# Attention value products as direct fp32 matmuls of 64 columns, low parts moved by DMA

## The chip, the cores and the metric

The kernel runs on one core of a Trainium2 chip. The metric is the time of the program on the device in microseconds (us). The core has a matrix engine (TensorE, PE in the rows; PEld is its weight loads), a vector engine (VectorE, DVE), a scalar engine (ScalarE, ACT), GpSimd (POOL), and SyncE (SP), which here only issues DMAs. Each engine executes its own list of instructions in order and waits on semaphores for the others.

## The reference

Two layers over 256 tokens of width 1024. Layer 0 is a gated linear recurrence, layer 1 attention; each is followed by a squared-ReLU MLP of width 4096. All is fp32. The change lies in layer 1:

```
proj  = h @ w_in                  # q (16 heads of 64), 6 k/v sets (4 groups of 64), 48 gates
k_c   = gelu(flat(k blocks) @ w1_k) @ w2_k          # "compressed" keys, 15 blocks of 32 tokens
v_c   = gelu(flat(v blocks) @ w1_v) @ w2_v
for each head h of group g (4 heads a group):
    p_c = softmax(q k_c^T - slope * distance)       # 15 columns
    p_s = softmax(q k_s^T - slope * distance)       # causal; all 4 blocks are selected
    p_w = softmax(q k_w^T - slope * distance)       # causal; the window covers all 256 tokens
    o_h = gate0 * p_c v_c + gate1 * p_s v_s + gate2 * p_w v_w
x = x + concat(o) @ w_out
```

## The kernel before

Everything is stored transposed: `xt` holds the residual as 8 chunks of 128 features by 256 tokens. An fp32 product is made of three fp32r products. An operand is split into a high part (a copy rounded to fp32r, `hi`) and a low part (the difference, `lo`), and `mm3` (L307) issues hi·hi, hi·lo and lo·hi into the same accumulator. The weights stream from HBM in 512 KB pieces into 5 raw buffers, are split by ScalarE (`whi`) and VectorE (`wlo`, L313), and are used once.

The attention layer is one `Section`: its parts call `add` with an engine, a planned duration, what they read and what they write, and a wished time `t`; `Plan.emit` (L202) orders them on every engine by list scheduling with those planned durations. So the order of the instructions is fixed when the kernel is built. `TSTAGE` and `FPS` set the wished times: one head every `TSTAGE` us, with `FPS` quarter-projections of "filler" work for TensorE between.

The section first makes the projections of the compressed branch (`cproj`), its hidden layer (`hidden`, L884: 96 matmuls with 64 weight columns and 62 streamed columns), the first keys (`kchunk`), the values of the two other branches (`values`) and the first queries (`qchunk`). Then 16 heads go through it:

- `scores` (L1050): products of queries and keys for the two query halves and both branches (128x256 and 128x512). VectorE adds the ALiBi matrix and takes the maximum (L1075); ScalarE takes the exponential with its row sum (L1078). The query tiles `sa` and `sb` hold the high part of one head in one half of the partitions and its low part in the other half, so one matmul over 128 partitions does both parts.
- `rescale` (L1082): VectorE turns the sum into gate/sum (L1087, L1088, L1090) and multiplies `pt` by it as a broadcast tensor (L1096).
- `transposes` (L1100): TensorE transposes the probabilities; ScalarE makes `pth` (L1111), VectorE the low part `ptl` (L1112).
- `pv` (L1116), once for two heads: the weight tile `vhl` holds the high and the low part of the values side by side (64 + 64 columns), and `pth` and `ptl` are streamed through it (L1138, L1140), beside the compressed branch (L1127). The two halves of the 128 output rows are added by a ScalarE copy and a VectorE add (L1144, L1147), and the sum is split into `oh` and `ol` for the output projection.

The query and key projections of the later heads and the first half of the output projection (`out_t`) are the fillers. The second half of the output projection and the first three pieces of the second MLP end the section.

Of the kernel before, what the change touches and what calls it, by code (L numbers as in the profile page):

```python
# [19 lines left out]
P = 128  # L20
# [11 lines left out]
NPT, NTH = 3, 4  # L32
TSTAGE, FPS = 4.4, 3.0
# [18 lines left out]
def weight_pieces():  # L52

    order = []
    order += [{"c": ("in", 8 + i), "y": ("in", i)}[k] for k, i in RG_ORDER if k != "g"]
    order += [("out", m) for m in range(8)]
    order += mlp_pieces(0)
    order += [("ck", 0), ("ck", 1), ("cv", 0), ("cv", 1), ("ks", 0), ("kw", 0), ("w1k", 0), ("w1v", 0)]
# [10 lines left out]
GATES = [("gate", i) for i in range(4)]  # L69
# [150 lines left out]
def trunk_kernel(ctx: ExitStack, tc: tile.TileContext, x_in, vec_in, const_in, w2_in, wts, out):  # L220
# [556 lines left out]
    with ExitStack() as ph:  # L777
# [18 lines left out]
        osumt = at.tile([P, 2, S], F32, name="osum")  # L796
        osum = [osumt[:, i] for i in range(2)]
# [3 lines left out]
        ptht, ptlt = (at.tile([P, NTH * 3 * P], F32R, name=n) for n in ("pth", "ptl"))  # L801
        pth, ptl = ([x[:, i * 3 * P:(i + 1) * 3 * P] for i in range(NTH)] for x in (ptht, ptlt))
        add("pool", 1.74, lambda e: e.memset(kl.bitcast(F32), 0.0), w=["kl"], t=-9)
        add("pool", 0.15, lambda e: e.memset(kc.bitcast(F32), 0.0), w=["kc0"], t=-9)

        ti = {"n": 0}

        def qchunk(c, b, t, step):
            z, zk = proj_t("q", c, b, t, step)
            t += 4 * step  # L810
            n = ti["n"] = ti["n"] + 1
            x, xk = tt[n % 3], ("tt", n % 3)
# [4 lines left out]
            add(HI, copy(a[:64], x[:64]), r=[xk], w=[ak], t=t + 0.5)  # L817
            add(HI, copy(b_[64:], x[64:]), r=[xk], w=[bk], t=t + 0.5)
            add("dve", 0.34, diff(a[64:], x[:64], a[:64]), r=[xk], w=[ak], t=t + 1)
            add("dve", 0.34, diff(b_[:64], x[64:], b_[64:]), r=[xk], w=[bk], t=t + 1)  # L820

        def kchunk(gp, br, b, t, step):
            z, zk = proj_t(("ks", "kw")[br], gp, b, t, step)
            t += 4 * step
            n = ti["n"] = ti["n"] + 1
            x, xk = tt[n % 3], ("tt", n % 3)
            add("dve", 0.34, lambda e: e.tensor_tensor(x, z(), rs, op=OP.mult), r=[zk, "rs"], w=[xk], t=t)
            cs = slice(br * S, (br + 1) * S)
            for hf in range(2):
                own, oth, g = own_(hf), own_(1 - hf), gp * 2 + hf  # L830
                gk = ("k", g, br)
                add(HI, copy(kh[own, g, cs], x[own]), r=[xk], w=[gk], t=t + 0.5)
                add(HI, copy(kh[oth, g, cs], x[own]), r=[xk], w=[gk + (1,)], t=t + 0.5)
                add("dve", 0.34, diff(kl[own, g, cs], x[own], kh[own, g, cs]), r=[xk, gk, "kl"], w=[gk + (2,)],
                    t=t + 1)
# [9 lines left out]
        zhs = [zv(oht, i * 4 * S) for i in range(2)]  # L845
        zls = [zv(olt, i * 4 * S) for i in range(2)]
        zpt = [[("pt", i, qc, b) for i in range(NPT) for qc in range(2) for b in range(2)]] * 2
        zok = [[(n, 4 * i + j) for n in ("oh", "ol") for j in range(4)] for i in range(2)]
        hvk = [(n, i) for n in ("pth", "ptl") for i in range(NTH)]
        w2h = pre.tile([64, 192], F32R, name="w2h")  # L850
        w2l = pre.tile([64, 192], F32R, name="w2l")
        cb = [pre.tile([64, 2], F32, name="cb%d" % i) for i in range(2)]
        hid = [pre.tile([64, 4, NCP], F32, name="hid%d" % i) for i in range(2)]
        hkh = pre.tile([64, 4 * NCP], F32R, name="hkh")
        hkl = pre.tile([64, 4 * NCP], F32R, name="hkl")
        hvh, hvl = (x[:64, :512].rearrange("p (a b f n) -> p a b f n", a=4, b=4, f=2) for x in (ptht, ptlt))
        bd = osumt.rearrange("p a (j e) -> p a j e", j=4)
        add("act", 0.25, copy(w2h, w2raw), w=["w2h"], t=2)
        add("dve", 0.3, diff(w2l, w2raw, w2h), r=["w2h"], w=["w2l"], t=2)
# [7 lines left out]
        def cproj(i, gp, b, t, step):  # L867
            z, zk = proj_t(("ck", "cv")[i], gp, b, t, step)
            t += 4 * step
            for hf in range(2):  # L870
                g = gp * 2 + hf
                own = own_(hf)
                dst = zfs[i][:, g * NB:(g + 1) * NB].rearrange("p n l -> p (n l)")
                for j in range(2):
                    add("dve", 0.34, lambda e, dst=dst, own=own, j=j: e.tensor_tensor(
                        dst[own_(j)], z()[own, j * 16:j * 16 + 240], rs[own, j * 16:j * 16 + 240], op=OP.mult),
                        r=[zk, "rs"], w=[("zf", i, g, j)], t=t + 0.1 * j)

        def csplit(i, t):
            keys = [("zf", i, g, j) for g in range(4) for j in range(2)] + [("zf", i, "p"), ("zf", i, "z")]  # L880
            add([("act", 0.95, 0.0), ("dve", 0.6, 0.5)], copy(zhs[i], zfs[i]), r=keys + zpt[i], w=[("zh", i)] + zok[i], t=t)
            add("dve", 1.1, diff(zls[i], zfs[i], zhs[i]), r=keys + zpt[i] + [("zh", i)], w=[("zl", i)] + zok[i], t=t)

        def hidden(i, b, t):  # L884
            wh, wl, wk = weight("w1k" if i == 0 else "w1v", 0, t)
            hp = zview(("hp", i), b, lambda x: x[:64])
            for q_ in range(4):
                def run(e, q_=q_):
                    for l in range(4 * q_, 4 * q_ + 4):
                        w = slice(l * 64, (l + 1) * 64)  # L890
                        mm3(hp()[:, :ZW], wh[:, w], wl[:, w], zhs[i][:, :, l], zls[i][:, :, l], l == 0, l == 15)
                add("pe", 0.61, run, r=wk + zok[i] + [("zh", i), ("zl", i)], w=[("ps", b)], t=t + 0.7 * q_)
            t += 3
# [5 lines left out]
        def kc_out(t):  # L899
            hf_ = hid[0].rearrange("p g n -> p (g n)")  # L900
            add("act", 0.2, copy(hkh, hf_), r=[("hid", 0)], w=["hkh"], t=t)
            add("dve", 0.15, diff(hkl, hf_, hkh), r=[("hid", 0), "hkh"], w=["hkl"], t=t)
            o = zview("kco", 6, lambda x: x[:, :4 * NCP])
            add("pe", 0.33, lambda e: mm3(o(), w2h[:, :P], w2l[:, :P], hkh, hkl, True, True),
                r=["w2h", "w2l", "hkh", "hkl"], w=[("ps", 6)], t=t)
            o4 = lambda: o().rearrange("p (g n) -> p g n", g=4)
            add("act", 0.1, lambda e: e.copy(kc[:, :, 0], o4()), r=[("ps", 6), "kc0"], w=["kch"], t=t)
            for hf in range(2):
                own = own_(hf)
                add("dve", 0.1, lambda e, own=own, hf=hf: e.tensor_tensor(  # L910
# [3 lines left out]
        def vc_out(t):  # L914
            bc = lambda g: hid[1][:, g, None, :].to_broadcast([64, 8, NCP])
            part = lambda x, g: x[:, g // 2 * 2:g // 2 * 2 + 2, :, g % 2].rearrange("p a b n -> p (a b) n")
            for g in range(4):
                add("act", 0.2, copy(part(hvh, g), bc(g)), r=[("hid", 1)] + hvk, w=[("hvh", g)], t=t)
                add("dve", 0.2, diff(part(hvl, g), bc(g), part(hvh, g)), r=[("hid", 1), ("hvh", g)] + hvk, w=[("hvl", g)],
                    t=t)  # L920
            o = zview("vco", 7, lambda x: x[:, :4 * 64].rearrange("p (a e) -> p a e", a=4))

            def run(e):
                for a in range(4):
                    lh, ll = (x[:, a].rearrange("p b f n -> p (b f n)") for x in (hvh, hvl))
                    mm3(o()[:, a], lh, ll, w2h[:, P:], w2l[:, P:], True, True)
# [423 lines left out]
```

## Time and profile before

| | |
|---|---|
| median of three timed runs | 605.43 us (605.3 to 605.85) |
| span of the profiled execution, first to last instruction | 602.2 us |
| what lies around the span (median less span) | 3.2 us |
| TensorE, VectorE, ScalarE busy | 96%, 75%, 59% of the span |
| weights read from HBM | 99.2 MB, mean 166 GB/s |
| attention section on TensorE | about 263 to 417 us, then the second MLP |

Busy times are sums over instructions. TensorE overlaps its matmuls, so the length of one (about 280 ns for 256 columns) is longer than the time to the start of the next (about 115 ns), and a wait that is shorter than the difference does not show as idle. The profiled execution's own total is not listed apart from its span; the 3.2 us around it are taken as fixed.

### The profile page before, as it was taken

The page shows a single profiled execution, that of the slowest core. Times are in us where ns is not written, and L with a number is a line of the kernel's source. Part 1 is how long each engine was busy: PE and PEld are TensorE (multiplying, and loading weights), DVE is VectorE, ACT ScalarE, POOL GpSimd, SP SyncE. Part 2 cuts the span into 40 slices and gives each one's busy share as a digit, 9 for nine tenths or more (in the row PEclk, how much of TensorE's full clock was granted, in tenths as well). Part 3 has the DMA queues.
Part 4 walks back from the last instruction along what each step waited for, and adds up shares of the span by engine and source line. Part 5 has one row for each costly group of instructions (what it writes and reads, how often), then busy time and mean ns, then how long its engine had stood idle before and what let it go on. Part 6 is the DMA issues. An engine that isn't in the chain of part 4 may idle for free.

```text
span 602.2 us, 12254 instructions
## 1 busy us (share of the span) xinstructions
PE 578.5 (96%) x4835; PEld 563.7 (94%) x4835; DVE 448.7 (75%) x921; ACT 355.0 (59%) x684; POOL 46.7 (8%) x57
## 2 busy tenths in 40 slices
PE   8999999999999999999999877899999999999994
PEld 7999999999999999999998765789999999999994
DVE  6999997767674564669999998999876667364432
ACT  7799586666563343446778766686666565253310
POOL 2110000000001221310010000000000000142220
PEclk9999999999999999999999988899999999999997
DMA  8933676555556556453730021116676667656402
GB/s 296 372 132 106 210 245 211 198 187 203 185 208 210 177 194 221 167 190 124 275 106 2 0 82 60 53 57 205 215 215 199 189 198 215 208 170 208 149 1 71
DMA packets 29178, 101.07 MB, mean 168 GB/s; under 512 B 3376, under 2 KB 4016, under 8 KB 29120
## 3 DMA queue, kind: packets, MB, share of 16 engines
q1 hardware_dynamic: 28512, 99.70, 50.0%
q8 instruction: 38, 0.62, 0.4%
q10 hardware_dynamic: 576, 0.53, 0.3%
q14 instruction: 20, 0.16, 0.1%
q0 software_dynamic: 32, 0.05, 0.0%
HBM read 99.22 MB, written 1.05 MB: 166 GB/s over the span
## 4 chain that ended last, share of the span: by engine, by line
PE 76%; DVE 19%; ACT 2%; issue 1%; DMA 1%; SPq 0%; DVEq 0%
PE bank L309 24%; PE bank L308 24%; PE bank L310 24%; DVE wlo L313 3%; DVE ptl L1112 2%; DVE pt L1096 2%; DVE pt L1075 2%; DVE xb L627 2%; DVE osum L1147 1%; DMA xt<-in_dram 1%; PE bank L950 1%; PE bank L951 1%; PE bank L952 1%; DVE t L679 1%; PE bank L1140 1%
## 5 line engine op out<-in xcount | busy, mean ns | idle before, releaser
L308 PE MATMUL bank<-hhl,whi 128*128 128x256 f32 x768 | 215.1, 280 | 1.9 <-DVE tt L815 1.0
L310 PE MATMUL bank<-hhl,wlo 128*128 128x256 f32 x768 | 213.0, 277 | 0.4 <-DVE wlo L313 0.4
L309 PE MATMUL bank<-hhl,whi 128*128 128x256 f32 x768 | 213.1, 277 | 0.1
L308 PEld LDWEIGHTS bank<-hhl,whi 128*128 128x128 f32 x768 | 144.6, 188 | 3.0 <-DVE tt L815 1.4
L277 DVE TENSOR_TENSOR wlo<-raw,whi 128x1024 fp32r<-128x1024 f32 x115 | 143.9, 1272 | 2.2 <-ACT whi L268 2.2
L310 PEld LDWEIGHTS bank<-hhl,wlo 128*128 128x128 f32 x768 | 144.4, 188 | 0.8 <-DVE wlo L313 0.8
L309 PEld LDWEIGHTS bank<-hhl,whi 128*128 128x128 f32 x768 | 144.5, 188 | 0.6 <-DVE hhl L540 0.3
L308 PE MATMUL bank<-uhl,whi 128*128 128x256 f32 x512 | 141.7, 277 | 0.0
L309 PE MATMUL bank<-uhl,whi 128*128 128x256 f32 x512 | 141.7, 277 | 0.0
L310 PE MATMUL bank<-uhl,wlo 128*128 128x256 f32 x512 | 141.6, 277 | 0.0
L268 ACT CAST whi<-raw 128x1024 fp32r<-128x1024 f32 x116 | 118.0, 1039 | 23.1 <-issue 18.8
L308 PEld LDWEIGHTS bank<-uhl,whi 128*128 128x128 f32 x512 | 96.2, 188 | 0.0
L310 PEld LDWEIGHTS bank<-uhl,wlo 128*128 128x128 f32 x512 | 96.1, 188 | 0.0
L309 PEld LDWEIGHTS bank<-uhl,whi 128*128 128x128 f32 x512 | 96.1, 188 | 0.0
L313 DVE TENSOR_TENSOR wlo<-raw,whi 128x1024 fp32r<-128x1024 f32 (+2 forms) x76 | 81.3, 1094 | 1.3 <-ACT whi L316 1.0
L490 DVE TENSOR_TENSOR xt<-xt,bank 128x256 f32<-128x256 f32 x40 | 16.1, 413 | 84.7 <-PE bank L310 84.7
L316 ACT CAST whi<-raw 128x1024 fp32r<-128x1024 f32 (+2 forms) x70 | 67.3, 974 | 10.1 <-DMA raw<-in_dram 4.2
L742 ACT ACTIVATE u<-t 128x256 f32<-128x256 f32 x64 | 26.7, 418 | 58.5 <-DVE t L737 58.5
L737 DVE SCALAR_TENSOR_TENSOR t<-bank,rstd 128x256 f32<-128x256 f32 x64 | 26.9, 423 | 44.3 <-PE bank L310 44.1
L1078 ACT ACTIVATE pt<-pt,mx 128x128 f32<-128x128 f32 (+1 forms) x64 | 28.9, 451 | 8.2 <-DVE mx L1075 7.4
L1228 ACT ACTIVATE xg<-xt,vec 128x256 f32<-128x256 f32 x8 | 4.1, 511 | 48.0 <-DVE xt L490 48.0
L460 POOL TENSOR_TENSOR acc<-xt 128x256 f32<-128x256 f32 x2 | 3.0, 1524 | 365.9 <-DVE xt L490 365.9
(206 smaller groups left out, 849.2 us busy)
## 6 DMA issues: line engine op xcount, KB each, us to landing
raw<-in_dram SPq DMA_DIRECT2D x175, 512.0 KB, 4.3
raw<-in_dram SPq DMA_DIRECT2D x4, 560.0 KB, 5.2
gw<-in_dram SPq DMA_DIRECT2D x4, 512.0 KB, 8.7
raw<-in_dram SPq DMA_DIRECT2D x6, 256.0 KB, 5.5
xt<-in_dram SPq DMA_DIRECT2D x4, 256.0 KB, 5.4
cst<-in_dram SPq DMA_DIRECT2D x1, 304.0 KB, 5.6
out_dram<-xg SPq DMA_DIRECT2D x2, 128.0 KB, 2.3
out_dram<-xg ACTq DMA_DIRECT2D x2, 128.0 KB, 2.4
```

The costliest lines, as they stand in the source:

```text
L268: (act.copy if eng is None else eng.tensor_copy)(hi_t[i % NSPL][:, :n], raw_t[i % NRAW][:, :n])
L277: (eng or dve).tensor_tensor(lo[:, :n], raw_t[i % NRAW][:, :n], hi[:, :n].bitcast(F32), op=OP.subtract)
L308: pe.matmul(ps, wh, xh, start=start, stop=False)
L309: pe.matmul(ps, wh, xl, start=False, stop=False)
L310: pe.matmul(ps, wl, xh, start=False, stop=stop)
L313: return lambda e: e.tensor_tensor(o, a, h.bitcast(F32), op=OP.subtract)
L316: return lambda e: (e.copy if e is act else e.tensor_copy)(o, a)
L490: dve.tensor_tensor(xt[:, m], xt[:, m], z, op=OP.add)
L627: add("dve", 0.4, lambda e, i=i: e.scalar_tensor_tensor(xb[m], x[:, i:i + S], cw(i, m), xb[m], op0=OP.mult, op1=OP.add), r=[xk], w=[bk], t=t)
L737: dve.scalar_tensor_tensor(t, z, 0.0, rs, op0=OP.max, op1=OP.mult)
L742: act.activation(u, t, AF.Square)
L1078: add("act", (0.39, 0.49)[qc], lambda e, row=row, j=j: e.activation(row, row, AF.Exp, bias=mx[:, j:j + 1], scale=-1.0, accum_out=sm[:, j:j ...
```

## The change

- The values stay fp32 (`vv`, `bd`) and are not split. `pv` multiplies fp32 by fp32 directly: for every step one matmul of 64 weight columns for the first head into output rows 0 to 63 and one for the second head into rows 64 to 127, in turn. A group of two heads is ten such matmuls (two compressed, four of 256 columns, four of 128). `ptl`, `vhl`'s low half, `osum` and the halves' addition are gone. Heads are taken in another order, so that a pair shares a query chunk.
- `rescale` multiplies each row of `pt` by a per-partition scalar, four instructions a head, on VectorE or ScalarE as the planner chooses. The gate is kept as 1 + exp(-x), and maximum and product are one instruction.
- Low parts of queries and keys are made over all 128 partitions in one VectorE instruction (`tl`) and put into the other half by DMA on SyncE (`move`): 48 small DMAs (60 or 64 KB) in all, 16 of which also lay out the compressed branch's input.
- The compressed branch's hidden layer and its second layer use direct fp32 matmuls (32 + 1 + 4 for 96 + 3 + 12); their two weight pieces come by DMA into tiles of their own and are not split.
- `TSTAGE` goes from 4.4 to 5.0 and `FPS` from 3.0 to 3.25, so the planner orders the whole section anew.

```diff
-TSTAGE, FPS = 4.4, 3.0
+TSTAGE, FPS = 5.0, 3.25
...
+        def move(o, i, r, w, t):
+            o, i = (x if x.dtype == F32 else x.bitcast(F32) for x in (o, i))
+            add("sp", 0.4, lambda e: e.dma_start(o, i), r=r, w=w, t=t, lag=2.2)
...
         def qchunk(c, b, t, step):
...
-            add(HI, copy(a[:64], x[:64]), r=[xk], w=[ak], t=t + 0.5)
-            add(HI, copy(b_[64:], x[64:]), r=[xk], w=[bk], t=t + 0.5)
-            add("dve", 0.34, diff(a[64:], x[:64], a[:64]), r=[xk], w=[ak], t=t + 1)
-            add("dve", 0.34, diff(b_[:64], x[64:], b_[64:]), r=[xk], w=[bk], t=t + 1)
+            add(HI, copy(a, x), r=[xk], w=[ak, ak + (1,)], t=t + 0.5)
+            add(HI, copy(b_, x), r=[xk], w=[bk, bk + (1,)], t=t + 0.5)
+            add("dve", 0.34, diff(l_, x, a), r=[xk, ak, ak + (1,)], w=[lk], t=t + 1)
+            move(a[64:], l_[:64], [lk], [ak + (1,)], t + 1.2)
+            move(b_[:64], l_[64:], [lk], [bk + (1,)], t + 1.2)
...
         def hidden(i, b, t):
...
-                        mm3(hp()[:, :ZW], wh[:, w], wl[:, w], zhs[i][:, :, l], zls[i][:, :, l], l == 0, l == 15)
+                        e.matmul(hp()[:, :ZW], w1[i][:, l * 64:(l + 1) * 64], zfs[i][:, :, l], start=l == 0, stop=l == 15)
...
         def rescale(s, t):
...
-                add("dve", (0.34, 0.6)[qc],
-                    lambda e, v=v, qc=qc, nk=nk: e.tensor_tensor(
-                        v, v, sm[:, 2 * qc:2 * qc + 2, None].to_broadcast([P, 2, nk]), op=OP.mult),
...
+                for b in range(2):
+                    j, o = 2 * qc + b, qc * 2 * P + b * nk
+                    row, c_ = pt[:, o:o + nk], sm[:, j:j + 1]
+                    add([("dve", (0.14, 0.21)[qc], 0.0), ("act", (0.31, 0.41)[qc], 0.15)], lambda e, row=row, c_=c_: (
+                        e.activation(row, row, AF.Identity, scale=c_) if e is act else
+                        e.tensor_scalar(row, row, c_, None, op0=OP.mult)), r=[("sm", s % 4, j)], w=[("pt", s % NPT, qc, b)],
+                        t=t + 0.2)
...
-                add("act", 0.37, lambda e, tp=tp, i=i: e.copy(pth[i], tp()), r=bk, w=[("pth", i)], t=t + 0.3)
-                add("dve", 0.47, lambda e, tp=tp, i=i: e.tensor_tensor(ptl[i], tp(), pth[i].bitcast(F32),
-                                                                       op=OP.subtract),
+                add([("act", 0.38, 0.0), ("dve", 0.47, 0.2)], lambda e, tp=tp, i=i: copy(pT[i], tp())(e), r=bk, w=[("pT", i)], t=t + 0.3)
...
+        def pv(j, t):
+            p, a, n0 = j // 4, j // 2, j % 2 * 4
...
+            def run(e):
+                two = lambda c0, w, y, **k: [e.matmul(o()[own_(hf), c0:], w(hf), y(hf), **k) for hf in range(2)]
+                two(0, lambda hf: bd[:, a, j % 2 * 2 + hf], lambda hf: pcs[a % 2], start=True, stop=False)
+                for b in range(2):
+                    y = lambda hf: pT[n0 + 2 * hf + b]
+                    two(0, lambda hf: vv[:, 0, b, 2 * p + hf], lambda hf: y(hf)[:, :S], start=False, stop=False)
+                    two(P, lambda hf: vv[:, 1, b, 2 * p + hf], lambda hf: y(hf)[:, S:], start=False, stop=b == 1)
+            add("pe", 2.4, run, r=[("pT", n0 + i) for i in range(4)] + [("bd", a), "bd0", ("pc", a % 2), ("pc0", a % 2)] +
+                [("v", h, b) for h in range(2) for b in range(2)], w=bk, t=t)
+            add([("act", 0.28, 0.0), ("dve", 0.34, 0.2)], lambda e: copy(oh[j], o())(e), r=bk, w=[("oh", j)], t=t + 2.4)
+            add("dve", 0.34, lambda e: diff(ol[j], o(), oh[j])(e), r=bk + [("oh", j)], w=[("ol", j)], t=t + 2.7)
```

The change also moves instructions on every engine. On TensorE, the first group of value products stands behind a stretch of key projection in both orders (`bank_4006` and `bank_3921` are its accumulator, `vhl` and `vv` the values). Before:

```order
L308 MATMUL bank_3993<-hhl,whi_89 128x256
L309 MATMUL bank_3993<-hhl,whi_89 128x256
L310 MATMUL bank_3993<-hhl,wlo_96 128x256
L1127 MATMUL bank_4006<-pc_3261,bhl 128x256 x2
L1140 MATMUL bank_4006<-pth,vhl 128x512
L1140 MATMUL bank_4006<-ptl,vhl 128x512
L1138 MATMUL bank_4006<-pth,vhl 128x2x128
L1138 MATMUL bank_4006<-ptl,vhl 128x2x128
```

and now, with the sizes as output rows by columns:

```order
L308 MATMUL bank_3871<-hhl,whi_87 128x256
L309 MATMUL bank_3871<-hhl,whi_87 128x256
L310 MATMUL bank_3871<-hhl,wlo_94 128x256
L1102 MATMUL bank_3921<-pc_3239,bd 64x256 x2
L1102 MATMUL bank_3921<-pT,vv 64x256 x2
L1102 MATMUL bank_3921<-pT,vv 64x128 x2
L1102 MATMUL bank_3921<-pT,vv 64x256 x2
L1102 MATMUL bank_3921<-pT,vv 64x128 x2
```

The group stands in the same place of the flow; each "x2" is the pair of the two heads, one for each half of the output rows.

On VectorE, the second head's rescaling (`sm` the sums, `pt` the probabilities) before, among the maximum and the compressed branch (`cm`, `cs`):

```order
L1090 TENSOR_TENSOR sm_3252<-sm_3252,gts 128x4
L1023 TENSOR_TENSOR cs_3255<-cs_3255,cst 128x128
L1024 TENSOR_REDUCE cm_3259<-cs_3255 128x8
L1112 TENSOR_TENSOR ptl<-bank_3916,pth 128x384
L1112 TENSOR_TENSOR ptl<-bank_3922,pth 128x384
L1025 TENSOR_SCALAR cm_3259<-cm_3259 128x8
L1096 TENSOR_TENSOR pt<-pt,sm_3252 128x512
L1096 TENSOR_TENSOR pt<-pt,sm_3252 128x256
```

and the first head's now:

```order
L1070 SCALAR_TENSOR_TENSOR sm_3253<-sm_3253,gts 128x4
L1001 TENSOR_TENSOR cs_3257<-bank_3799,cst 128x128
L1072 RECIPROCAL sm_3253<-sm_3253 128x4
L1080 TENSOR_SCALAR pt<-pt,sm_3253 128x128
L1080 TENSOR_SCALAR pt<-pt,sm_3253 128x256 x2
L1002 TENSOR_REDUCE cm_3261<-cs_3257 128x8
```

The two large `ptl` instructions are gone from the row, and the wide products have become narrower ones with a scalar; the fourth of this head stands on ScalarE.

On SyncE, the small DMAs stand among the weight loads (`raw`) in one list; this is where the second half of the keys and the fifth query chunk are put in place (before, only `raw` rows stood here):

```order
L254 DMA raw_80<-in_dram 128x1024
L823 DMA kh<-kh 64x256
L823 DMA kl<-tl_3229 64x256
L823 DMA kh<-kh 64x256
L823 DMA kl<-tl_3229 64x256
L823 DMA kl<-tl_3227 64x256
L823 DMA kh<-kh 64x256
L823 DMA kl<-tl_3227 64x256
L254 DMA raw_81<-in_dram 128x1024
```

A small DMA that waits for its source holds the weight loads behind it, and the reverse.

## Rows read from the trace of the kernel before

**Rows 1.** Stretches of the section: length, busy per engine, PEclk, DMA share, GB/s
```profile
263.20:303.00 39.80, 39.80 (x380) 39.44 (x379) 37.07 (x71) 27.77 (x46) 2.48 (x8) 1.00 0.57 190
350.00:390.00 40.00, 30.72 (x178) 26.14 (x177) 37.46 (x140) 25.70 (x75) 0.00 (x0) 0.87 0.18 54
303.00:417.20 114.20, 101.09 (x697) 89.78 (x696) 110.08 (x388) 81.52 (x234) 1.71 (x4) 0.96 0.21 66
```
**Rows 2.** Chain of waits from 303 to 417.2 us, shares by line
```profile
by line: DVE ptl L1112 11.0%; DVE pt L1096 9.1%; DVE pt L1075 9.0%; DVE wlo L313 8.1%; DVE osum L1147 5.0%; PE bank L309 4.5%; PE bank L308 4.5%; PE bank L310 4.3%; issue 3.1%; PE bank L1140 3.1%; DVE sa L313 3.0%; DVE sb L313 2.6%; ACT pt 
```
**Rows 3.** VectorE groups, 303 to 417.2 us: busy us, mean ns, idle before
```profile
L1112 DVE TENSOR_TENSOR ptl<-bank,pth 128x384 fp32r<-128x384 f32 x32 | 17.1, 547 | 0.2
...
L1096 DVE TENSOR_TENSOR pt<-pt,sm 128x512 f32<-128x512 f32 x16 | 10.9, 684 | 0.1
...
L1147 DVE TENSOR_TENSOR osum<-osum,bank 64x256 f32<-64x256 f32 x16 | 6.7, 417 | 1.5 <-ACT osum L1144 1.2
L1096 DVE TENSOR_TENSOR pt<-pt,sm 128x256 f32<-128x256 f32 x16 | 6.6, 413 | 0.0
...
L313 DVE TENSOR_TENSOR sb<-tt,sb 64x256 fp32r<-64x256 f32 x8 | 3.4, 420 | 0.2
...
L1087 DVE TENSOR_SCALAR sm<-sm 128x4 f32<-128x4 f32 x16 | 2.6, 161 | 0.0
```
**Rows 4.** VectorE prices of single-input forms, whole span
```profile
L316 DVE CAST kh<-tt 64x256 fp32r<-64x256 f32 x4 | 1.2, 289 | 0.1
...
L316 DVE CAST whi<-raw 128x1024 fp32r<-128x1024 f32 x1 | 0.7, 680 | 0.0
...
L977 DVE TENSOR_SCALAR gts<-gts 128x96 f32<-128x96 f32 x1 | 0.2, 199 | 0.0
```
**Rows 5.** ScalarE groups, 303 to 417.2 us
```profile
L316 ACT CAST whi<-raw 128x1024 fp32r<-128x1024 f32 x15 | 15.6, 1042 | 1.9 <-PE bank L309 1.1 <-DMA raw<-in_dram 0.9
...
L1078 ACT ACTIVATE pt<-pt,mx 128x128 f32<-128x128 f32 x32 | 12.7, 398 | 4.1 <-DVE mx L1075 3.6
...
L1144 ACT COPY osum<-bank 64x256 f32<-64x256 f32 x16 | 5.9, 366 | 3.9 <-PE bank L1138 3.7
```
**Rows 6.** TensorE in order of time: start, us, what; one group of value products
```profile
391.91 0.40 PE L1127 MATMUL bank<-pc,bhl 128*128 128x256 f32 x2
...
393.55 0.39 PE L1068 MATMUL bank<-kh,sb 128*128 128x512 f32 x1
...
394.01 0.28 PE L308 MATMUL bank<-oh,whi 128*128 128x256 f32 x1
...
394.70 0.49 PE L1108 MATMUL bank<-cst,pt 128*128 128x128 f32 x3
394.94 0.36 PE L308 MATMUL bank<-oh,whi 128*128 128x256 f32 x1
```
**Rows 7.** TensorE in order of time, direct fp32 matmuls of layer 0
```profile
27.13 1.89 PE L647 MATMUL bank<-xb,gw 128*128 128x256 f32 x8
```
**Rows 8.** Line 647: durations min/median/max (ns), records
```profile
L647 PE MATMUL bank<-xb,gw x64: 378/380/380, 27.1 to 43.5; 128*128 128x256 f32 x64
```
**Rows 9.** TensorE in order of time, the norm's spread and the hidden layer
```profile
269.14 0.61 PE L487 MATMUL bank<-cst,rcol 128*128 128x128 f32 x4
...
280.49 0.21 PE L308 MATMUL bank<-oh,whi 128*64 128x62 f32 x1
...
286.06 0.39 PE L950 MATMUL bank<-whi,hhl 128*128 128x304 f32 x1
```
**Rows 10.** DMA issues: KB each, median us from issue to landing
```profile
raw<-in_dram SPq DMA_DIRECT2D x175, 512.0 KB, 4.3
...
out_dram<-xg SPq DMA_DIRECT2D x2, 128.0 KB, 2.3
```
**Rows 11.** Line 254 on SyncE's queue: duration of an issue, ns
```profile
L254 SPq DMA_DIRECT2D raw<-in_dram x179: 327/328/617, 6.0 to 564.6; - x179
```

More of the change, by code (lines that the diff above doesn't have):

```diff
@@ L31 @@
 NRAW, NSPL = 5, 7
[L32 to L33 removed]
+NPT, NTL = 3, 3
+TSTAGE, FPS = 5.0, 3.25
 CST = (0.5, 4.0, 8.5, 12.0)
@@ L66, in weight_pieces @@
     return order
-GATES = [("gate", i) for i in range(4)]
+EXTRA = [("gate", i) for i in range(4)] + [("w1k", 0), ("w1v", 0)]
 def mlp_pieces(i):
@@ L829, in kchunk @@
             for hf in range(2):
+                g = gp * 2 + hf
+                add(HI, copy(kh[:, g, cs], x), r=[xk], w=[("k", g, br), ("k", g, br, 1)], t=t + 0.5)
+            add("dve", 0.34, diff(l_, x, kh[:, gp * 2, cs]), r=[xk, ("k", gp * 2, br), ("k", gp * 2, br, 1)], w=[lk], t=t + 1)
+            for hf in range(2):
                 own, oth, g = own_(hf), own_(1 - hf), gp * 2 + hf
[L831 to L835, printed above, removed]
+                move(kh[oth, g, cs], kh[own, g, cs], [("k", g, br)], [("k", g, br, 1)], t + 0.8)
+                move(kl[own, g, cs], l_[own], [lk, "kl"], [("k", g, br, 2)], t + 1.2)
         def kkeys(g, br):
@@ L844, in trunk_kernel @@
         zfs = [zv(ptt, i * ZW * 16) for i in range(2)]
[L845 to L851, printed above, removed]
+        zpt = [("pt", i, qc, b) for i in range(NPT) for qc in range(2) for b in range(2)]
         cb = [pre.tile([64, 2], F32, name="cb%d" % i) for i in range(2)]
         hid = [pre.tile([64, 4, NCP], F32, name="hid%d" % i) for i in range(2)]
[L854 to L859, printed above, removed]
+        hv = pre.tile([64, 4, 2, 2, NCP], F32, name="hv")
         for i in range(2):
@@ L869, in cproj, with hidden @@
             t += 4 * step
+            x, xk, _, _ = turn()
+            add("dve", 0.34, lambda e: e.tensor_tensor(x, z(), rs, op=OP.mult), r=[zk, "rs"], w=[xk], t=t)
             for hf in range(2):
                 g = gp * 2 + hf
-                own = own_(hf)
                 dst = zfs[i][:, g * NB:(g + 1) * NB].rearrange("p n l -> p (n l)")
                 for j in range(2):
[L875 to L879, printed above, removed]
+                    move(dst[own_(j)], x[own_(hf), j * 16:j * 16 + 240], [xk], [("zf", i, g, j)], t + 0.4)
+        def hidden(i, b, t):
+            hp = zview(("hp", i), b, lambda x: x[:64])
             keys = [("zf", i, g, j) for g in range(4) for j in range(2)] + [("zf", i, "p"), ("zf", i, "z")]
[L881 to L886, printed above, removed]
             for q_ in range(4):
@@ L987, in trunk_kernel @@
         css, cs2, cmx = many([P, 4, 2, NCP], F32, "cs", 2), many([P, 2, 4, NCP], F32, "cq", 2), many([P, 8], F32, "cm", 2)
-        pcs = many([P, S], F32R, "pc", 2)
-        heads = [(p, 2 * cp + i, hf) for p in range(2) for cp in range(2) for hf in range(2) for i in range(2)]
+        heads = [(p, c, hf) for p in range(2) for c in range(4) for hf in range(2)]
         sbank = [2, 3, 4]
@@ L1007, in run @@
                                  start=True, stop=True)
-            xk = [(n, (2 * a + j) % NQ) for n in ("sa", "sb") for j in range(2)]
+            xk = [(n, (2 * a + j) % NQ) + k for n in ("sa", "sb") for j in range(2) for k in ((), (1,))]
             add("pe", 0.76, run, r=xk + ["kch", ("kcl", 0), ("kcl", 1)], w=b7, t=t)
@@ L1274, in _arrange @@
     wo = f["nsa_w_out"][0]
-    perm_o = [h * 64 + e for p in range(2) for cp in range(2) for g in (2 * p, 2 * p + 1)
-              for h in (g * 4 + 2 * cp, g * 4 + 2 * cp + 1) for e in range(64)]
-    wo = wo[perm_o]
+    wo = wo[perm]
     w1 = {"w1k": f["nsa_w1_k"][0], "w1v": f["nsa_w1_v"][0]}
@@ L1304, in piece @@
         return np.concatenate([_chunk(w, 2 * i), _chunk(w, 2 * i + 1)], axis=1)
-    wts = np.concatenate([np.ascontiguousarray(piece(n, i)).reshape(-1) for n, i in weight_pieces() + GATES])
+    wts = np.concatenate([np.ascontiguousarray(piece(n, i)).reshape(-1) for n, i in weight_pieces() + EXTRA])
     h = np.arange(1, NH + 1, dtype=np.float64)
```

145 lines of the change are left out of this document (49 added, 96 removed).

## The prediction

> **What bounds the kernel now.** I read the stretches first. Outside the attention section TensorE is busy all the time, and no instruction there is touched, so the question is what paces the section, from 263.2 to 417.2 us. Up to 303 us it is TensorE: busy 39.80 of 39.80 us [rows 1]. From 303 us, when the heads begin, it is VectorE: 110.08 of 114.20 us, 96%, against 101.09 for TensorE and 81.52 for ScalarE [rows 1]. TensorE is idle 13.1 us there, and from 350 to 390 us its mean granted clock is 0.87: 10.4 us at the lower of its two levels (1.2 instead of 2.4 GHz), which costs 5.2 us more. The chain of waits says the same: its first five entries are VectorE's, led by the low part of the probabilities (L1112, 11.0%) and the rescaling (L1096, 9.1%) [rows 2]. Both are what the change rewrites. So a VectorE microsecond saved in this stretch is a microsecond saved, until TensorE, which gets more work, takes over.
>
> **VectorE, 303 to 417 us.** Removed: `ptl`, 32 x 0.547 = 17.5 us; the broadcast rescaling, 10.9 + 6.6 = 17.5; the addition of the halves, 6.7; one of the three small operations per head, 2.6; and of the 64-partition operations (0.42 each) 14: eight of sixteen low parts of the queries, two of four for the keys, four of the compressed branch, 5.9 [rows 3]. Sum 50.2. Added: 47 of the 64 multiplications by a scalar (23 of 128 columns, 24 of 256; 17 go to ScalarE). No row shows this form at these sizes. Single-input forms show 0.199 for 96 columns and 0.289 for 256 [rows 4]; I take 0.21 and 0.28, together 11.6. The upper bound is the two-input price, 0.413 for 256 columns [rows 3] and half of that for 128, 14.7; the lower, 0.16 for each [rows 3], 7.5. Seven weight copies that the planner moves here from ScalarE cost 7 x 0.68 = 4.8 [rows 4], two copies of transposed probabilities at the price of `ptl` 1.1, casts 0.3. Net 50.2 - 17.8 = 32.4 less: VectorE needs 77.7 us of the stretch.
>
> **ScalarE** loses 16 copies for the halves (5.9 us) and nine weight copies (9 x 1.04 = 9.4), gains 17 multiplications (at 0.40 for 128 columns and some 0.47 for 256, 7.3), and loses some ten half-tile casts (4): 81.5 becomes about 69.5 [rows 1, 5]. It is no bound.
>
> **TensorE, what stays.** Its 101.1 busy us less the 5.2 of the lower clock and less the value products (below, 13.1) leave 82.8. That still holds waits too short to show as idle. Counted by starts at the full clock it is less: 225 projection and 192 output matmuls at 0.115 (six in 0.69 us), 48.0; score products at 0.23 and 0.115 (the two before 394.01 take 0.46), 32 of each, 11.0; 96 transposes at 0.08, 7.7; 40 small ones of the compressed branch at the same price, 3.2 [rows 6]. Sum 69.9. So the work that stays is between 69.9 (no hidden wait) and 82.8 (all of them). VectorE causes part of the hidden waits, in-order hand-over between engines the rest; I take the middle, 76.4.
>
> **TensorE, the value products.** Before, one group runs from 391.91 to 393.55, 1.64 us, and eight take 13.1 [rows 6]. Now a group is six matmuls of 256 columns and four of 128, in direct fp32. The trace has this kind in layer 0: 32 matmuls leave 64 records of 380 ns [rows 8], two a matmul, and eight records spread over 1.89 us start (1.89 - 0.38)/7 = 0.216 us apart [rows 7]. So one of 256 columns takes 0.43 and one of 128 0.215. One after the other a group is 6 x 0.43 + 4 x 0.215 = 3.45 us, 27.6 for eight. But each pair writes separate output rows from separate halves of the array's columns. If the two halves of a pair run side by side, a group takes half, 1.73, or 13.8 for eight. No row shows matmuls in turn on two halves: the hidden layer's 64-column matmuls before all use the same half. The fp32 row stands no nearer to one end than to the other, so I take the middle, 2.6 a group and 20.8 for eight, and keep both ends.
>
> **Sum for the stretch.** 76.4 + 20.8 = 97.2 us of TensorE work, above VectorE's 77.7: TensorE is now the bound. With 1.5 us idle left (first scores, last output) 98.7 instead of 114.2: -15.5.
>
> **The first stretch**, to 303 us, is TensorE's already. The hidden layer goes from 280.49 to 286.06, 96 matmuls 0.058 apart [rows 9]. Now there are 32 with two records each: at the same spacing 3.7 us, -1.9. The bounds are 3.0 (fp32 price by columns, 0.093) and 7.4 (four times 0.058), so -2.6 to +1.8. The second layers go from 15 matmuls to 5 of two records, -0.6. Together -2.5.
>
> **Where I cost an edit at nothing.** The 48 DMAs: SyncE issues in order, 0.33 us each [rows 11], and a small transfer onto a quiet queue lands after 2.3 us, a weight piece after 4.3 [rows 10]. The compressed branch's inputs can be written after the norm's spread; that comes some 18 matmuls (2 us) later in the new order than the 269.14 of [rows 9]. Three copies, twelve issues (4 us) and a landing end about 279 us, before the hidden layer at some 280.2. If they land like a weight piece, TensorE waits 1 to 2 us once. Query chunk 0 has 42 matmuls (4.8 us) between its last product and the first scores; copy, cast, low part, two issues and landing need 0.42 + 0.29 + 0.42 + 0.66 + 2.3 = 4.1. The later chunks have 6 us or more. A weight load queued behind a waiting move is late only if five buffers run empty; the DMA share of this stretch is 0.21 [rows 1]. The scheduler's `TSTAGE` sets only priorities; its order is what the bounds on waits allow for.
>
> **Total.** 602.2 - 15.5 - 2.5 = 584.2 us of span, plus the 3.2 around it: **587.4 us**.
>
> **Rivals.**
> *Halves side by side.* The value products take 13.8: 76.4 + 13.8 + 1.5 = 91.7 us, a total of 580.4. For it: separate columns and output rows in every pair. Against it: each matmul brings two weight loads for only 64 columns. With no hidden wait as well, 69.9 + 13.8 + 1.5 = 85.2, total 574. The Trainium skill (TensorEngine Tiling (Array Packing), Tiling Modes) says that tiles of 64 columns load weights and multiply independently, for up to a factor of 2. That is this rival's time; no run here shows it yet.
>
> *Strictly one after the other.* 27.6: 76.4 + 27.6 + 1.5 = 105.5, total 594.2. For it: records of one line elsewhere never overlap beyond their tails.
>
> *The waits pass on.* TensorE's hidden waits are hand-over and stay (82.8), the halves run in turn (27.6), and idle of 3 us remains: 113.4, total 602. For it: in-order queues and three score banks. Against it: VectorE falls from 96% to under 80% of the stretch.
>
> *Slower: the array drains between the halves.* If a matmul of one half only starts when the other half's has left the array, every record costs its whole length: 12 x 0.38 [rows 8] and 8 x about 0.28 (the difference of 64 columns twice) make 6.8 us a group, 54.4 for eight. Then 76.4 + 54.4 + 1.5 = 132.3, total 621. It decides as soon as a group takes more than (114.2 + 2.5 - 77.9)/8 = 4.9 us. The same page (Key Properties) says that a change of mode drains the engine, a change of tile not; by that the drain comes only at a group's two ends.
>
> *The change not doing what it says*: a multiplication by a scalar that costs the two-input price adds 3.1 us to VectorE, 80.8, still under TensorE.
>
> **Chances.** Middle case 40%, side by side 20%, one after the other 18%, waits pass on 10%, drain or another slowdown 10%, no change otherwise 2%. This measurement can tell about 0.2%, 1.2 us. Faster: 40 + 20 + 18 and 9 of the 10 for passed-on waits, 87%; within 0.2% 3%; slower 10%. The range from 576 to 600 leaves out the slow case, the far end of passed-on waits and the best corner.
>
> **What would show it.** In the new profile: VectorE under 85 us of busy time from the first scores to the last output product, and no longer first in the chain there; the clock at its full level in that stretch; a group of ten value matmuls from first to next start between 1.7 and 3.5 us; `pt` multiplications of 0.2 and 0.28 us on VectorE; no wait of TensorE on a small DMA above 2 us. I am wrong if a group takes over 4.9 us, if TensorE waits for moves at many heads, or if its waits for ScalarE replace those for VectorE.

## The result and the profile after

The changed kernel takes **582.41 us** (581.79 to 583.51, four runs) against 605.37 for the kernel before beside it: a ratio of 0.9618, 95% interval 0.9604 to 0.9631. Forecast were 587.4, range 576 to 600. The profiled execution's span is 581.1 us, 21.1 less than before; in all runs of the changed kernel 1.7 to 1.8 us lie around the span.

TensorE is in the section from 263.8 to 395.9 us, 132.1 us instead of 154.0. The cut at 304 us is put where the order stands about as far as at 303 us before; six more projection matmuls (231 for 225, 0.7 us) fall behind it. Same columns as [rows 1]; the third row begins at the first scores (310.18 us, before 306.59):

```profile
263.80:304.00 40.20, 39.84 (x336) 38.78 (x335) 23.29 (x41) 17.48 (x26) 3.95 (x11) 1.00 0.69 215
304.00:395.90 91.90, 91.80 (x783) 84.03 (x783) 85.94 (x335) 74.66 (x230) 1.93 (x4) 1.00 0.36 109
310.20:395.90 85.70, 85.60 (x729) 77.83 (x728) 80.46 (x324) 71.06 (x224) 0.00 (x0) 1.00 0.36 109
```

TensorE now has hardly any idle time, and its clock is granted at the full level (1.00) all through. The second stretch is 22.3 us shorter than its counterpart of [rows 1], the first 0.4 us longer. The chain of waits from 304 to 395.9 us has turned over against [rows 2]: TensorE leads with eight entries, VectorE's first is 2.6%.

```profile
by line: PE bank L308 17.0%; PE bank L309 16.0%; PE bank L310 15.8%; PE bank L1102 14.3%; PE bank L1091 10.9%; PE bank L1050 5.1%; PE bank L1051 5.0%; PE bank L990 2.8%; DVE pt L1057 2.6%; DVE pt L1080 2.1%; ACT pt L1060 1.5%; PE bank L1027
```

A group of value products in order of time, as in [rows 6]: ten matmuls, which leave 20 records, from 373.62 to the next start at 375.50, 1.88 us instead of 1.64.

```profile
373.62 0.65 PE L1102 MATMUL bank<-pc,bd 128*64 128x256 f32 x4
374.10 1.47 PE L1102 MATMUL bank<-pT,vv 128*64 128x256 f32 x16
375.50 0.39 PE L308 MATMUL bank<-oh,whi 128*128 128x256 f32 x1
```

The hidden layer, as in [rows 9]: 3.55 + 0.95 + 2.69 us (start to the next start of another line) for 64 records, 7.2 us instead of 5.57.

```profile
281.19 3.61 PE L890 MATMUL bank<-pt,w 128*64 128x62 f32 x32
284.74 0.41 PE L940 MATMUL bank<-whi,hhl 128*128 128x304 f32 x1
...
286.90 1.02 PE L890 MATMUL bank<-pt,w 128*64 128x62 f32 x8 [0.36 <-issue]
287.85 0.43 PE L900 MATMUL bank<-hid,w2raw 64*128 64x64 f32 x2
288.21 2.76 PE L890 MATMUL bank<-pt,w 128*64 128x62 f32 x24
290.90 0.41 PE L940 MATMUL bank<-whi,hhl 128*128 128x304 f32 x1
```

VectorE groups from 304 us on (columns of [rows 3]): the multiplication by a scalar (L1080) is dearer than taken from [rows 4], and six weight copies (`whi`) came over from ScalarE.

```profile
L313 DVE TENSOR_TENSOR wlo<-raw,whi 128x1024 fp32r<-128x1024 f32 x15 | 18.2, 1220 | 1.2 <-ACT whi L316 1.2
...
L1080 DVE TENSOR_SCALAR pt<-pt,sm 128x256 f32<-128x256 f32 x24 | 8.0, 348 | 0.1
...
L1080 DVE TENSOR_SCALAR pt<-pt,sm 128x128 f32<-128x128 f32 x23 | 6.1, 281 | 0.3
...
L316 DVE CAST whi<-raw 128x1024 fp32r<-128x1024 f32 x6 | 4.1, 685 | 0.0
```

The DMAs that the change adds (KB each, median us from issue to landing, as in [rows 10]):

```profile
w<-in_dram SPq DMA_DIRECT2D x2, 512.0 KB, 6.0
pt<-tt SPq DMA_DIRECT2D x16, 60.0 KB, 3.1
kh<-kh SPq DMA_DIRECT2D x8, 64.0 KB, 3.8
kl<-tl SPq DMA_DIRECT2D x8, 64.0 KB, 3.2
sb<-tl SPq DMA_DIRECT2D x8, 64.0 KB, 2.0
sa<-tl SPq DMA_DIRECT2D x8, 64.0 KB, 2.1
```

### The profile page after: what moved, and what is told of

Same layout as the page of the kernel before. It is cut to its first block, busy times and chain, and to the rows that moved or that the text cites. A ratio compares the mean times of both kernels' runs of the same rounds, so it can differ in the third digit from the quotient of the medians.

```text
span 581.1 us, 12312 instructions
## 1 busy us (share of the span) xinstructions
PE 570.3 (98%) x4878; PEld 558.7 (96%) x4878; DVE 408.7 (70%) x834; ACT 335.4 (58%) x655; POOL 48.3 (8%) x60
## 4 chain that ended last, share of the span: by engine, by line
PE 89%; DVE 8%; issue 1%; DMA 1%; ACT 1%; DVEq 0%
PE bank L308 26%; PE bank L310 26%; PE bank L309 26%; PE bank L1102 2%; PE bank L1091 2%; DVE xb L627 2%; DVE wlo L313 2%; PE bank L890 1%; PE bank L1050 1%; PE bank L940 1%; PE bank L1051 1%; PE bank L941 1%; PE bank L942 1%; DMA vec<-in_dram 1%; DVE t L679 1%
## 5 line engine op out<-in xcount | busy, mean ns | idle before, releaser
L313 DVE TENSOR_TENSOR wlo<-raw,whi 128x1024 fp32r<-128x1024 f32 (+2 forms) x74 | 79.6, 1096 | 5.4 <-ACT whi L316 5.0
L316 ACT CAST whi<-raw 128x1024 fp32r<-128x1024 f32 (+2 forms) x61 | 58.1, 964 | 14.2 <-PE bank L942 4.5
```

The source lines that it names most:

```text
L313: return lambda e: e.tensor_tensor(o, a, h.bitcast(F32), op=OP.subtract)
L316: return lambda e: (e.copy if e is act else e.tensor_copy)(o, a)
```

## Experiments

Theory A says: VectorE's work was the bound; without it TensorE sets the end; and the direct fp32 products cost TensorE no more than before because matmuls on the two halves run side by side. Each experiment has its own rivals. The changes to the kernels are shown shortened, partly in words. Times are medians; "against the changed kernel" is the difference to 582.4 us.

**The two halves one after the other**

```diff
-   for each step: matmul of head 0, matmul of head 1       # five steps
+   five matmuls of head 0, then five of head 1
```

> The changed kernel, but each group of value products issues the five matmuls of the first head and then the five of the second, instead of in turn; the planner sees the same task, so nothing else moves. Theory A (matmuls on the two halves of the columns run side by side, and only because they are neighbours): a group goes from 1.78 us to 12 x 0.216 + 8 x 0.11 = 3.5 us, eight groups +13.6 us, total 596; if the weight loads (0.053 us each) are no longer hidden either, up to 604. Rival B (an fp32 matmul of 64 weight columns simply costs half as much as one of 128, whatever stands beside it): 582.4, no change.

Measured: 591.47 us (ratio to before 0.9758, 0.9745 to 0.9772), 9.1 us slower than the changed kernel, whose group takes 1.88 us (the expectation has 1.78). The last of its groups but one, in order of time (L1104 compressed, L1107 256 columns, L1108 128 columns):

```profile
379.08 0.65 PE L1104 MATMUL bank<-pc,bd 128*64 128x256 f32 x2
...
380.22 0.38 PE L1107 MATMUL bank<-pT,vv 128*64 128x256 f32 x1
380.22 0.43 PE L1104 MATMUL bank<-pc,bd 128*64 128x256 f32 x1
380.43 0.38 PE L1107 MATMUL bank<-pT,vv 128*64 128x256 f32 x1
380.49 0.38 PE L1104 MATMUL bank<-pc,bd 128*64 128x256 f32 x1
...
382.10 0.39 PE L308 MATMUL bank<-oh,whi 128*128 128x256 f32 x1
```

The group takes 379.08 to 382.10, 3.02 us instead of 1.88, and 8 x 1.14 = 9.1 is the whole loss. Rival B is out: the pairs make the price, and here a microsecond on TensorE is a microsecond of the total. A's 3.5 us a group was too much, and the rows show why: at 380.22 the second head's first matmul (L1104) starts together with one of the first head's last four, so where the heads meet they overlap after all. In the changed kernel's trace the two records of a pair start 0.006 us apart, and the next pair follows 0.22 us behind one of 256 columns.

**More work on VectorE**

```diff
             reciprocal(sm)
+            subtract(spare, cst, cst)     # 128x384; once, and twice in the second kernel
```

> The changed kernel, with one subtraction of 128x384 on VectorE added behind the reciprocal of each head (16 in all; its result is not used). Before, the low part of the probabilities of this size cost 0.547 us, so this adds about 8.8 us to VectorE's 85.9 us in the 91.9 us from the first scores to the end of the section. Theory A (TensorE is the bound now, VectorE 6 us below it): VectorE's 94.7 us pass it by 2.8; total 585 to 589. Rival B (VectorE still paces the heads and each microsecond on it counts): +8.8, total 591. Rival C (VectorE is far off the path): 582.4.

> As the kernel with one added subtraction for each head, but with two: 17.5 us more VectorE work, what the low parts of the probabilities had cost. Theory A: VectorE's 103.4 us set the stretch in place of 91.9; +11.5 and some of the old idle time, total 594 to 598. Rival B (each VectorE microsecond counts already): +17.5, total 600. Rival C (off the path): 582.4. A and B differ by the 6 us of room that A gives VectorE.

Measured: 586.98 us (0.9694, 0.9681 to 0.9708) and 596.79 us (0.9849, 0.9835 to 0.9862): 4.6 and 14.4 us slower. From the first scores to the section's end, of the first and of the second kernel:

```profile
310.10:400.40 90.30, 87.71 (x729) 78.17 (x728) 86.58 (x340) 71.21 (x224) 0.00 (x0) 1.00 0.34 104
```

```profile
309.50:408.90 99.40, 89.46 (x729) 78.38 (x728) 95.31 (x356) 71.10 (x224) 0.00 (x0) 1.00 0.31 94
```

VectorE is the bound again in both, busy 95.9% of the stretch, the same 96% as in [rows 1]. So C is out, and no kernel here has VectorE busier than 96%. By that the changed kernel's 80.46 us need 83.8 of its 85.7: the room is about 2 us, not 6 (the 85.9 of 91.9 us of the expectation begin at 304 us, not at the first scores). A's bounds held, but the free part is small, so A and B lie close together: in busy time the subtractions add 6.1 and 14.9 us, and the stretch grows by 4.6 and 13.7. At 96% they alone would need 6.4 and 15.5, so B is out by 1.8 us in both.

**No rescaling at all**

```diff
-                    (four multiplications of pt by sm, on VectorE or ScalarE)
```

> The changed kernel without the rescaling multiplications: the probabilities go to the transposes as the exponential left them (the factor gate/sum is still computed and not used), so the output is not the reference's. VectorE's work in the heads' stretch falls by 14.1 us, ScalarE's by 7.7. Theory A (TensorE's own work sets the end): what the two give back is only TensorE's short waits, at most the 7 us between the 91.9 us of the stretch and the 84.9 us that its matmuls take by their starts; 577 to 581. Rival B (VectorE at 94% busy is the real limit): -10 or more, 572 or less.

Measured: 582.74 us (0.9626, 0.9610 to 0.9642): no change. From 310 us on:

```profile
310.00:395.60 85.60, 85.60 (x729) 77.72 (x728) 74.25 (x285) 62.39 (x200) 0.00 (x0) 1.00 0.36 110
```

VectorE falls from 80.46 to 74.25 us and ScalarE from 71.06 to 62.39, and the stretch stays at 85.6. (VectorE falls by 6.2 and not by the 14.1 taken out: the planner moved four copies of transposed probabilities and some casts to it.) Rival B is out, and so is the part of A that expected short waits to come back. With this much less on both engines TensorE's own list takes as long as before.

**The old rescaling**

```diff
-                    tensor_scalar(row, row, sm[:, j])            # or ScalarE, four a head
+                tensor_tensor(v, v, sm.to_broadcast(...))        # VectorE, two a head
```

> The changed kernel with the old rescaling: two VectorE multiplications by a broadcast tensor for each head (0.413 and 0.684 us, 17.5 us in all) in place of 47 multiplications by a scalar on VectorE (14.1 us) and 17 on ScalarE (7.7 us). VectorE's work in the stretch of the heads rises by 3.4 us, from 85.9 to 89.3. The kernel with 8.4 us of added VectorE work came out 4.6 us slower, so some 4 us are free. Theory A (TensorE sets the end; VectorE's first 4 us are free): 582 to 584. Rival B (the rescaling was a part of the gain by itself, and each microsecond of it counts): 586 or more.

Measured: 582.26 us (0.9613, 0.9599 to 0.9628): no change, in A's range. Its groups from 304 us on show the old prices back:

```profile
L1077 DVE TENSOR_TENSOR pt<-pt,sm 128x512 f32<-128x512 f32 x16 | 11.0, 685 | 0.1
...
L1077 DVE TENSOR_TENSOR pt<-pt,sm 128x256 f32<-128x256 f32 x16 | 6.7, 417 | 0.2
```

17.7 us for 14.1. VectorE does not rise, however (busy 80.42 us from the first scores): the planner gave the six weight copies (4.1 us) back to ScalarE. So VectorE's room was not put to the test, and this run does not tell A from B; it shows that the planner makes up for the old rescaling, and that the new one earned nothing here.

**Halves placed by the engines**

```diff
-            copy(a, x); copy(b_, x); l_ = x - a                 # 128 partitions
-            dma(a[64:], l_[:64]); dma(b_[:64], l_[64:])
+            copy(a[:64], x[:64]); copy(b_[64:], x[64:])         # likewise for the keys
+            a[64:] = x[:64] - a[:64]; b_[:64] = x[64:] - b_[64:]
```

> The changed kernel, but the low parts and copies of queries and keys are written into the other half of the partitions by VectorE and ScalarE again, two half-tile operations each, in place of one full one and 32 DMAs. VectorE gets 12 more operations of 0.42 us, 5.0 us, of which 4.2 in the stretch of the heads. Theory A (TensorE sets the end, the DMAs are hidden and so worth nothing but the VectorE time): 582 to 584. Rival B (TensorE or the queue of SyncE loses time to the DMAs' landing, 2 to 4 us each): faster, 579 to 581.

Measured: 585.98 us (0.9671, 0.9656 to 0.9685), 3.6 us slower. Neither number was met. B is out by sign: whatever the 32 DMAs cost, it is less than placement by the engines. From the first scores on:

```profile
307.70:399.20 91.50, 90.16 (x752) 81.24 (x753) 85.71 (x332) 77.54 (x236) 0.00 (x0) 1.00 0.27 83
```

VectorE has 5.25 us more than in the changed kernel, ScalarE 6.5 more, and TensorE is idle 1.3 us. With 2 us of room 5.25 more would cost about 3.3, close to the 3.6. But this does not show that VectorE is the bound: the stretch also holds 23 TensorE records more (2.6 us), VectorE is busy 93.7% of it and not 96%, and what part ScalarE has was not told apart. Why the 3.6 us are lost stays open.

**The direct products alone, in the kernel before**

```diff
 # kernel before
-   pth, ptl; vhl, bhl (high and low part); osum and the halves' addition
+   pT, vv, bd in fp32; ten direct matmuls a group, the two heads in turn
```

> The kernel before with one part of the change alone: values and transposed probabilities stay fp32, the products are the direct fp32 matmuls on the two halves, and the low parts and the addition of the halves go. Rescaling, placement of the halves, hidden layer and the planner's settings stay as before. VectorE's 110.1 us in the stretch fall by 17.5 (low parts of the probabilities), 6.7 (addition) and 1.7 (low part of the compressed branch) to about 84 to 85. Theory A (this part alone brings VectorE below TensorE, which then sets the end): nearly the whole gain, 582 to 586, where the fp32r hidden layer even saves 1.5 us. Rival B (the gain goes with the VectorE time saved, 25.9 of some 32): 588. Rival C (the gain needs the placement by DMA or the new rescaling): 592 or more.

Measured: 585.62 us (0.9670, 0.9656 to 0.9685) against 605.87 beside it: 20.2 us of the changed kernel's 23.0. C is out. From its first scores on, and its chain there:

```profile
306.70:399.90 93.20, 89.21 (x754) 80.84 (x753) 89.82 (x335) 74.09 (x219) 0.00 (x0) 1.00 0.26 83
```

```profile
by line: DVE pt L1066 14.1%; DVE pt L1087 12.6%; PE bank L308 7.7%; PE bank L309 7.4%; PE bank L310 7.4%; DVE wlo L313 6.3%; PE bank L1112 6.1%; DVE sb L313 3.6%; DVE sa L313 3.2%; PE bank L1099 3.1%; DVE tt L817 2.5%; ACT pt L1069 2.2%; is
```

The time is within A's 582 to 586, but the mechanism is B's, though its 588 is missed by 2.4: this kernel is still bound by VectorE, at 96% (89.82 of 93.20), and the stretch followed it. From the first scores on VectorE fell by 16.9 us (before 106.68), less than the 25.9 expected, and the stretch by 17.4. So the rest of the change is worth the last 3.2 us only, from VectorE's bound to TensorE's.

**The planner's settings, both ways**

```diff
 # kernel before               # changed kernel
-TSTAGE, FPS = 4.4, 3.0        -TSTAGE, FPS = 5.0, 3.25
+TSTAGE, FPS = 5.0, 3.25       +TSTAGE, FPS = 4.4, 3.0
```

> The kernel before with only the planner's two settings changed (a head every 5.0 us instead of 4.4, 3.25 quarter projections of filler instead of 3.0). Theory A (VectorE's work sets the end of that stretch, so another order of the same work changes little): 603 to 608. Rival B (a good part of the gain is the new order, which fits the clock's and the engines' needs better): 600 or less.

> The changed kernel with the planner's two settings of the kernel before (a head every 4.4 us, 3.0 quarter projections of filler). The kernel before with the new settings came out 1.9 us faster. Theory A (the same work in another order; TensorE's work and VectorE's at 96% busy set the stretch): 581 to 585. Rival B (the new order is needed for the gain): 587 or more.

Measured: 603.96 us (0.9969, 0.9952 to 0.9986) and 583.59 us (0.9641, 0.9625 to 0.9656). The new settings are worth 1.9 us in the kernel before; in the changed one the 1.2 is not clear of noise, as its interval overlaps the changed kernel's. A holds in both.

**The two hidden layers in pairs**

```diff
-   for l in 0..15: matmul(hp0, w1k[l], zk[l]);  later  for l in 0..15: matmul(hp1, w1v[l], zv[l])
+   for l in 0..15: matmul(hp[:64], w1k[l], zk[l]); matmul(hp[64:], w1v[l], zv[l])
```

> The changed kernel, but the two hidden layers of the compressed branch are issued in turn, one matmul of the keys' layer into output rows 0 to 63 and one of the values' layer into rows 64 to 127 (62 streamed columns each); the same 32 matmuls. Theory A (halves run side by side, weight loads too): the 7.1 us of 64 records become about 3.6, and as TensorE is busy all the time there, total 579. Rival B (records this short are paced by their issue, 0.107 us each wherever they go): 582.4.

> The changed kernel with the two hidden layers issued in turn on the two halves, as in the kernel that gained 1.4 us and showed TensorE waiting 1.2 us after the first of these matmuls, and with the planner told that the DMAs that bring their inputs land 4.0 us later instead of 2.2, so that other work stands ahead of them. Theory A (64 records at 0.107 us become pairs at 0.107, and the wait was the inputs' landing): 3.4 us less than the changed kernel, 579. Rival B (the wait moves elsewhere, to the second layers or the first heads, or the heads' stretch gives it back since VectorE is nearly full there): 581 to 582.

> As the kernel with paired hidden layers and the later landing, and with the planner's costs set to what the trace of the changed kernel shows: a group of value products 1.88 us instead of 2.4, a multiplication by a scalar 0.28 and 0.35 us on VectorE instead of 0.14 and 0.21, and 0.40 and 0.50 on ScalarE. Theory A (the planner gives more multiplications to ScalarE, which is 83% busy, and VectorE falls below the 94% that it has in the heads' stretch): 577 to 579. Rival B (TensorE sets the end whatever the order): as the kernel without the new costs, 579 to 580.

Measured: 580.98 (0.9590, 0.9577 to 0.9603), 581.14 (0.9594, 0.9577 to 0.9612) and 580.21 us (0.9592, 0.9569 to 0.9615; its runs lie between 578.71 and 582.52). TensorE in order of time, of the first:

```profile
283.68 0.41 PE L893 MATMUL bank<-pt,w 128*64 128x62 f32 x2
284.98 3.63 PE L893 MATMUL bank<-pt,w 128*64 128x62 f32 x62 [0.90 <-issue]
288.54 0.41 PE L944 MATMUL bank<-whi,hhl 128*128 128x304 f32 x1
```

The 62 records take 284.98 to 288.54, 3.56 us: 0.115 for a pair, against 0.111 for a single record in the changed kernel (3.55 for 32). That is side by side a second time, with other sizes, and B is out. But only the first keys' matmul could start; the values' first stands 1.2 us behind it, and the last DMA of its inputs landed 0.4 us before that. In the second kernel that wait is gone, and one of the same kind stands in front of the compressed scores (third column: idle before, and what ended it):

```profile
L994 PE MATMUL bank<-kc,sa 128*128 128x32 f32 x16 | 2.6, 241 | 1.1 <-DMA sa<-tl 1.1
```

There the rival on moved waits was right. In the third kernel, with the measured costs, ScalarE makes 25 of the 64 multiplications (16 in the second, 17 in the changed kernel), and the total is near that of its rival B; TensorE waits 0.7 us for `sa` there. The first kernel is 1.4 us faster than the changed one, its interval just apart from the changed kernel's; for the other two this measurement cannot tell. All three gain less than the 3.6 us that the pairs take off TensorE; where the rest goes in the third is not shown.

## Why the prediction was right, and where it was off

The outcome and the mechanism were right: VectorE bounded the heads, TensorE takes over, and the clock comes back (1.00 instead of 0.96). The time lies 5.0 us under the forecast. The steps below add up to -5.3; besides, the section begins 0.6 us later and what follows it takes 0.2 more, and the median lies 0.4 under the profiled execution. By its steps:

- **TensorE, the value products: mis-sized.** 2.6 us a group was the middle between two ends, because the fp32 row "stands no nearer to one end than to the other". The end of the first rival is the right one: 1.88 a group, 2.05 for the first, 15.2 for eight instead of 20.8 (-5.6). One head after the other, the group is 3.02, not 3.45, as they overlap where they meet. What speaks for the halves was in the text (separate columns and output rows in every pair); I gave it 20%. The rule of the Trainium skill (TensorEngine Tiling (Array Packing), Tiling Modes), that tiles load and multiply independently, agrees with the 1.88 against 3.02 us.
- **TensorE, what stays: right in size, its reason wrong.** 91.9 - 15.2 = 76.7 us, forecast 76.4. But the part above the count by starts (69.9) is not the rescaling's doing: without the multiplications nothing of it came back. The count itself was low. By start-to-start sums the weight products take 2.2 us more than counted and the six that came over the cut 0.7, the transposes 9.7 instead of 7.7, the compressed branch's small ones 4.2 instead of 3.2, the scores 12.0 instead of 11.0; that is all of it. The 0.08 us for a transpose is a misreading: it was taken from a group of three, where the last one's step is 0.03 and the others' 0.11, and the weight product behind it then takes 0.20. In a group of six it is 0.57 / 6 = 0.095, and with the product's 0.21 each comes to 0.11:

```profile
329.83 0.82 PE L1091 MATMUL bank<-cst,pt 128*128 128x128 f32 x6
330.40 0.36 PE L308 MATMUL bank<-hhl,whi 128*128 128x256 f32 x1
330.61 0.28 PE L309 MATMUL bank<-hhl,whi 128*128 128x256 f32 x1
```

- **Idle time:** 0.1 us instead of 1.5 (-1.4).
- **The first stretch: wrong sign.** +0.4 instead of -2.5, and +1.1 if the six projection matmuls are counted where they stood before. The hidden layer took 7.2 us, near its upper bound of 7.4, not 3.7: a direct fp32 record of 62 columns takes 0.107 to 0.111 us, twice the 0.058 of the fp32r records of [rows 9] that I carried over, though both kinds use one half alone. That is 3.5 us, and the second layers' gain is lost in it. (The lower bound was wrong too: by columns 0.43 x 62/256 is 0.104 a matmul, not 0.093.)
- **VectorE: 85.9 us instead of 77.7.** It still was not the bound, so the total didn't feel it, but the margin was near nothing. Three causes make up the 8.2. The multiplications cost 0.281 and 0.348 instead of 0.21 and 0.28 (that of 128 columns is above my upper bound of half the two-input price): 14.8 us by durations instead of 11.6. Of the weight splits (`wlo`), the additions to `xt` and the norm 3.5 us more fall into the new stretch, against one weight copy fewer (-0.7). And I subtracted durations from busy time. The busy time of the rows is no sum over instructions: it counts a moment once, and neighbouring instructions overlap. In the stretch before, count times mean over all groups makes 135 us in 110 busy, now 109 in 86, so 2.3 us of what was taken out had been hidden. ScalarE has 74.7 instead of 69.5, above all because twelve of its fifteen weight copies stay and not six. The sign "VectorE under 85 us" from the first scores is met (80.46), and it does not lead the chain; the sign of 0.2 and 0.28 us a multiplication is not.
- **The DMAs at nothing: right in the heads, nearly so ahead of them.** They land in 2.0 to 3.8 us (medians by tile; the longest 7.2), no wait of TensorE for them shows among the heads, and giving the work of 32 of them to the engines brings no time back. But an issue takes some 0.46 to 0.69 us and not the 0.33 of [rows 11]. The sixteen of the compressed branch, with one of 1.8 us among them:

```profile
L823 SPq DMA_DIRECT2D pt<-tt x16: 461/594/1806, 273.3 to 284.4; - x16
```

  The last of them lands at 286.4 us, where I had about 279. The values' hidden layer starts at 286.90, after the 0.36 us of idle time in its row above; projections that the order puts between the two hidden layers cover the rest. And the cover is thin: in two of the kernels with paired hidden layers TensorE waits 1.1 and 0.7 us for `sa`.
- **Around the span:** 3.2 us was no constant. All runs of the changed kernel have 1.7 to 1.8; of the kernel before, runs beside the experiments have 1.7 to 1.9, with spans of 602.1 to 604.7. So the profiled execution of 602.2 us was some 1.5 us quicker than the median of its kernel. This term is 1.5 of the 5.0.

Of the rivals, side by side came true (580.4 against 582.4); one after the other, waits that pass on, and the drain did not. That its 91.7 us for the stretch are so near the 91.9 is in part luck: 1.4 us more for the products and 1.4 less idle time cancel.

What each part earned: the direct products 20.2 us of 23.0 by themselves; placement by DMA 3.6 when it is undone, the new order some 1.2 (not clear of noise), the rescaling 0. They do not add up, as the bound changes hands on the way. The direct hidden layer, the other order of heads and the merged small operations were not undone by themselves; by the trace the hidden layer costs TensorE 1.6 us more than before.

## What to carry to other kernels

When an engine is at 96% in a stretch, subtract the work from it only down to the next engine's own time, and price that one by starts, not by busy shares. Where a matmul needs only 64 weight columns, give the other half to a neighbour: two independent direct fp32 products cost here about as much as one. And after the hand-over, test by leaving work out: a kernel without the multiplication told in one run that nothing more was to be had from the rescaling.

## What the runs showed of the hardware

- Two direct fp32 matmuls of 64 columns, one on each half, run side by side: 20 records in 1.88 us in turn, 3.02 by head. The two records of a pair start 0.006 us apart. They need not be issued strictly in turn: a record of the second half started while four of the first half's were still to run.
- A direct fp32 record of 62 streamed columns on one half costs 0.111 us (3.55 for 32), a pair on both halves 0.115 (3.56 for 31).
- No kernel here has VectorE beyond 96% of a stretch: 96.4% and 96.4% in two kernels that it bounds, 95.9% in the two with added work.
- Multiplying by a per-partition scalar costs 0.281 us for 128 columns and 0.348 for 256, a copy of 256 columns with rounding 0.285 to 0.292.
- Issuing a DMA of 60 or 64 KB between two SBUF tiles holds SyncE 0.46 to 0.69 us (one 1.8), a weight piece from HBM 0.33 (median).
